# A hybrid encoder block on one NeuronCore: attention copies, query transposes and casts in another order, and a softmax factor made on GpSimd instead of VectorE

## The chip, the cores and the metric

The kernel runs on one core of one Trainium2 chip. The metric is the device time of one execution in microseconds (us), median of three runs.

## What is computed

One layer of a residual block on 512 rows of 1024 values, all in float32 (cut to what matters here):

```
h = rmsnorm(x);  z = h @ W_in            # MLA latents | differential q | k | v
# differential attention, 4 heads of 128, q and k in two maps of 64 each:
logits = q_m . k_m * scale + bias        # m = 0, 1, block-causal mask
probs  = softmax(logits)
attn   = probs[0] - lam * probs[1]
o      = rmsnorm(attn @ v) * (1 - lam_init)
x += concat[MLA heads (8 x 64), differential heads (4 x 128)] @ W_out
x += W_down( silu(causal_conv3(h2 W_gate)) * (h2 W_up) ),  h2 = rmsnorm(x)
x += sigmoid(rmsnorm(x) W_pg) * (p W_pp)
```

The two maps of a differential head are combined before they are multiplied by the values. With e0, e1 the exponentials and s0, s1 their sums over the keys, the kernel forms e0 + e1 * cf with cf = -lam * s0 / s1. That is s0 times the wanted row; the norm that follows removes the factor s0.

## The kernel before, in words

Every matrix product is made three times in reduced-precision float32: each operand is split into a high part (a cast, on ScalarE, line 185 or 150) and a low part (a subtraction, on VectorE, line 186 or 151), and `mm3` (lines 157 to 159) multiplies high by high, high by low and low by high.

TensorE's instructions run in the order in which the code issues them, through the whole kernel. VectorE, ScalarE and GpSimd run in the code's order only inside two regions (`tc.manual_schedule`); between the regions a scheduler of the framework orders them. The first region reaches from the first loads to just before the loop over the differential steps; that loop itself, `for i, (h, t) in enumerate(dslots)`, lies outside it. `tc.issue_after(x)` keeps an instruction behind x.

The stages: projections, then the MLA heads in four pairs `hp`, each in four steps `t` of 128 queries and (t+1)*128 keys, then the differential heads `h` in four steps `t` likewise, then the rest of W_out, the feed-forward part and the gate. While attention waits, TensorE is filled with units of other products: `pump(n)` takes the next n units of `zd_units` (the differential q, k and v) or, later, of `wo_units` (W_out).

An MLA step: `mla_logits` (maxima on VectorE), `mla_exp` (ScalarE), `mla_norm` (sums inverted, P scaled, VectorE), `mla_T` (P transposed on TensorE, then copied from PSUM to SBUF by VectorE or ScalarE, in `probs_T`), `mla_pv` (P times values). At the end of a pair the next pair's first logits follow at once.

A differential step (h, t): `diff_logits` makes the two maps' logits in two PSUM banks out of three (`lg`); VectorE adds the bias, writes the map into one of four SBUF buffers (`pmd`) and finds its row extreme in the same instruction (line 733, shown in the trace as CUSTOM_DVE_ANT_0, here called the maximum), and ScalarE makes the exponential with its sum (line 734). `diff_comb` makes the factor cf and combines the maps (lines 742 to 744). Logits and combination of step i+2 are issued in step i; then `probs_T` transposes step i's map and ScalarE copies it, and `diff_pv` multiplies step i-1 by its values. `diff_T(h, 0)` and `diff_T(h, 1)` transpose a head's queries and keys (TensorE, into one of two banks `tp`) and split them; `y_split` does so for a finished head.

The tiles of W_out are loaded into one of three buffers by SP's queue, cast, and split; a load can start when the low part of the tile that had the buffer is made. `first_hi` loads and casts the first tile in the MLA part (a table `extra` says at which step), `wo_units` the others.

Of the kernel before, what the change touches and what calls it, by code (L numbers as in the profile page):

```python
# [94 lines left out]
def hybrid_block(ctx: ExitStack, tc: tile.TileContext, a: dict, out: bass.AP):  # L95
# [27 lines left out]
    def pt_tile(name):  # L123
        return att.tile([P, T], F32, tag="pt", bufs=2, name=name)
# [10 lines left out]
    def small(name, shape, pool=None):  # L135
        return (pool or atts).tile(shape, F32, name=name)
# [3 lines left out]
    def load_raw(src, n, name):  # L140
        raw = wp["rawpool"].tile([P, 1024], F32, tag="raw", bufs=wp["raw"], name=f"raw_{name}")
        nc.sync.dma_start(raw[:, :n], src)
        return raw
# [51 lines left out]
    V.memset(ones, 1.0)  # L195
    mhalf = small("mhalf", [P, 32], keep)
    V.memset(mhalf, -0.5)
    S.activation(warm[:, :1], ones[:, :1], AF.Exp)
    wps = bank("ob", "warm")
    for i in range(WARM):  # L200
# [199 lines left out]
    def z_flush():  # L400
        while zouts:
            zouts.pop(0)()
# [137 lines left out]
    pump(FILL_QK)  # L540


    def probs_T(pm, n, name, on_act):

        ps = bank("tp", f"pT{name}")
        for j in range(0, n, P):
            TE.transpose(ps[:, j:j + P], pm[:, j:j + P], ident)
        pt = pt_tile("pt")
        if on_act:
            S.copy(pt[:, :n], ps[:, :n])  # L550
        else:
            V.tensor_copy(pt[:, :n], ps[:, :n])
        return pt
# [17 lines left out]
    def mla_logits(hp, t):  # L571

        n, one = (t + 1) * P, t < 2
        r = rq[:, 0, t, 2 * hp:2 * hp + 2]
        sums = sm.tile([P, 3, 2], F32, tag="sums", bufs=4, name="sums")
        nm = sums[:, 0]
        ps, pm = [], []
        for c in range(2):
            qh_, ql_, kh_, kl_ = QT[c]
            if c and one:  # L580
                ps.append(full[:, n:2 * n])
            else:
                full = bank("lg", f"ml{hp}{t}{c}")
                ps.append(full[:, :n])
            mm3(ps[c], [(qh_[:100, tsl[t]], ql_[:100, tsl[t]], kh_[:100, :n], kl_[:100, :n])])
            if not one:
                V.reduce_max(nm[:, c:c + 1], ps[c], axis=AX.X, negate=True)
                V.tensor_tensor(nm[:, c:c + 1], nm[:, c:c + 1], r[:, c:c + 1], op=ALU.mult)
        if one:
            V.reduce_max(nm, full[:, :2 * n].rearrange("p (c k) -> p c k", c=2), axis=AX.X, negate=True)  # L590
            V.tensor_tensor(nm, nm, r, op=ALU.mult)
        mla["lg", hp, t] = ps, nm, r
        for c in range(2):
            if c and one:
                pm.append(pmf[:, n:2 * n])
            else:
                pmf = pm_tile("pm")
                pm.append(pmf[:, :n])
        mla["pm", hp, t] = pm, pmf, sums, one

    def mla_exp(hp, t, c):

        ps, nm, r = mla["lg", hp, t]
        pm, pmf, sums, one = mla["pm", hp, t]
        S.activation(pm[c], ps[c], AF.Exp, bias=nm[:, c:c + 1], scale=r[:, c:c + 1], accum_out=sums[:, 1, c:c + 1])
# [10 lines left out]
    def mla_T(hp, t):  # L616

        n = (t + 1) * P
        pm, pmf, sums, one = mla.pop(("pm", hp, t))
        if one:  # L620
            pt = probs_T(pmf, 2 * n, f"m{hp}{t}", t)
            mla["pt", hp, t] = [pt[:, :n], pt[:, n:2 * n]]
        else:
            mla["pt", hp, t] = [probs_T(pm[c], n, f"m{hp}{t}{c}", c) for c in range(2)]

    def mla_pv(hp, t):

        if t == 0:
            mla["po"] = bank("ob", f"mo{hp}")
        po, pt = mla["po"], mla.pop(("pt", hp, t))  # L630
        for j in range(t + 1):
            for c in range(2):
                TE.matmul(po[64 * c:64 * c + 64, tsl[t]], kv[j][:, 2 * hp + c, 96:], pt[c][:, tsl[j]], start=j == 0, stop=j == t)
        if t == NT - 1 and hp < H // 2 - 1:
            yn = tt(f"ym{hp}")
            S.copy(yn, po)
            ymn.append(yn)
# [53 lines left out]
    def wo_units(kq, dqs, nk):  # L691

        for dq in dqs:
            w = wo_w(kq, dq)
            if kq == 0 and dq + 1 in dqs:
                with tc.issue_after(df["comb"].ins):
                    wo_first[0, dq + 1] = wo_w(0, dq + 1)
            if kq:
                wo2[dq] = w
            steps = [(b, k) for b in (2 * dq, 2 * dq + 1) for k in range(0, nk, 2)]  # L700
            if (kq, dq) == (0, 0):
                steps.sort(key=lambda s: s[1])
            ps = {}
            for b, k in steps:
                if k == 0:
                    ps[b] = bank("acc", f"o{kq}{b}")
                mm3(ps[b], wo_blocks(4 * kq + k, 4 * kq + k + 2, b, w), k == 0, k == nk - 2)
                if k == nk - 2:
                    add_x(b, ps[b])
                yield  # L710
# [27 lines left out]
    def diff_comb(h, t):  # L738

        pms, n, s0, s1 = df["pm", h, t]  # L740
        cf = sm.tile([P, 1], F32, tag="cf", bufs=4, name="cf")
        V.reciprocal(cf, s1)
        V.scalar_tensor_tensor(cf, cf, nlam, s0, op0=ALU.mult, op1=ALU.mult)
        df["comb"] = V.scalar_tensor_tensor(pms[0][:, :n], pms[1][:, :n], cf, pms[0][:, :n], op0=ALU.mult, op1=ALU.add)
        df["pm", h, t] = pms[0]

# [51 lines left out]
    z2_ = []  # L798
    z2_lo = lambda kq: lo(*z2_[kq])

    def first_hi():
        raw = load_raw(a["w_out"][0, 0], 1024, "o00")
        w = [wts.tile([P, 1024], F32R, tag=i, bufs=NW, name=f"{i}_o00") for i in ("hi", "lo")]
        wo_first[0, 0] = w
        z2_.append((*hi(raw, w[0]), w[1]))

    sq, zs = (lambda c, t: lambda: zd_sq(c, t)), (lambda c, t: lambda: zd_scale(c, t))
# [5 lines left out]
        5: [zl(1), sq(0, 3), lambda: zd_root(0)],  # L813
        6: [sq(1, 0), zh(2)],
        7: [zl(2), zh(3)],
        8: [zl(3), sq(1, 1), zs(0, 0), first_hi],
        9: [zl(4), sq(1, 2)],
        10: [sq(1, 3), lambda: zd_root(1), zs(0, 1)],
        11: [zs(0, 2), zs(0, 3)],
        12: [load_x, zs(1, 0), zs(1, 1)],  # L820
        13: [zs(1, 2), zs(1, 3)],
    }
    late = {
        14: [yy(0)],
        15: [yy(1)],
    }
    mla_q(0)
    pump()
# [11 lines left out]
    for hp in range(HP):  # L840
        for t in range(NT):
            i = NT * hp + t
            last = hp == HP - 1
            n = FILL_MLA[hp][t]
            if t:
                mla_norm(hp, t)
            if t < NT - 1:
                mla_logits(hp, t + 1)
            if t == 2:
                for c, (d, m) in enumerate(((diff_T, (0, 0)), (diff_T, (0, 1))) if last else ((mla_q, (2 * hp + 2,)), (mla_k, (2 * hp + 2,)))):  # L850
                    d(*m)
                    mla_exp(hp, t + 1, c)
            elif t < 2:
                for c in range(2):
                    mla_exp(hp, t + 1, c)
            else:
                pump()
                n -= 1
                if last:
                    diff_logits(0, 0)  # L860
                else:
                    mla_q(2 * hp + 3)
                    mla_k(2 * hp + 3)
            if t == 0:
                mla_norm(hp, t)
            for e in extra.get(i, ()):
                e()
            pump(n)
            for e in late.get(i, ()):
                e()  # L870
            mla_T(hp, t)
            z_flush()
            if i:
                mla_pv(*divmod(i - 1, NT))
            if t == 3 and not last:
                mla_logits(hp + 1, 0)
                for c in range(2):
                    mla_exp(hp + 1, 0, c)
    assert next(fill[0], None) is None
    fill[:] = [wo_units(0, range(4), 4)]  # L880
    diff_logits(0, 1)
    mla_pv(HP - 1, NT - 1)
    y_hl(3, mla["po"])
    diff_comb(0, 0)
    diff_T(1, 1)
    y_hl(2, ymn[2])
    diff_comb(0, 1)
    region.__exit__(None, None, None)
    pump()
    for i, (h, t) in enumerate(dslots):  # L890
        if i + 2 < len(dslots):
            diff_logits(*dslots[i + 2])
            diff_comb(*dslots[i + 2])
        pump(FILL_DIFF[h][t])
        df["pt", h, t] = probs_T(df.pop(("pm", h, t)), (t + 1) * P, f"d{h}{t}", True)
        if i:
            diff_pv(*dslots[i - 1])
        if h + 1 < DH and t == 0:
            diff_T(h + 1, 0)
        if h and t == 1:  # L900
            df["scaling"]()
        if t == 3 and h + 2 < DH:
            diff_T(h + 2, 1)
        if h and t == 2:
            y_split(4 + h - 1, df["y", h - 1], ocol, "tp")
        if h and t == 3:
            if h == 2:
                fill.append(wo_units(1, range(2), 2))
# [660 lines left out]
```

## Time and profile before

| what | value |
|---|---|
| median of three runs | 644.52 us (644.42 to 644.86) |
| the profiled execution | 644.82 us, of which the span is 643.0 us |
| TensorE busy in the span | 632.4 us (98%) |
| VectorE busy | 486.9 us (76%) |
| ScalarE busy | 360.2 us (56%) |
| GpSimd busy | 69.2 us (11%) |
| stretch of the differential heads | 157 to 217 us |

Times in the profile are counted from the span's start. In a row of the timeline the first number is the start, the second the duration, both in us; in a row of groups the two numbers behind the bar are the busy time in us and the mean duration of one instruction in ns. PE is TensorE, DVE VectorE, ACT ScalarE, POOL GpSimd, SP the queue of loads. [...]

### The profile page before, as it was taken

The numbers are of one execution on the slowest core, as the hardware profiler recorded it, in microseconds if no ns is written. First come the engines' busy times: TensorE is split into PE (matmuls) and PEld (weight loads), VectorE is DVE, ScalarE is ACT, GpSimd is POOL, SyncE is SP. The second block draws the span as 40 slices with busy tenths as digits, with TensorE's granted clock in tenths as the row PEclk, the third lists the DMA queues.
The fourth block names the chain that finished last, engine by engine and source line by source line (L and its number), as shares of the span: only waits on it lengthen the run. The fifth ranks groups of instructions, "written<-read, shape, count | busy, mean of one in ns | idle before, by whom it ended". The sixth has DMA issues, their size and how long they took to land.

```text
span 643.0 us, 10203 instructions
## 1 busy us (share of the span) xinstructions
PE 632.4 (98%) x3900; PEld 556.2 (87%) x3900; DVE 486.9 (76%) x870; ACT 360.2 (56%) x629; POOL 69.2 (11%) x94
## 2 busy tenths in 40 slices
PE   8999999999999999999999999999999999999997
PEld 8988888876777887889999999999999999988886
DVE  6889667887898678988876767676767777759844
ACT  7896567666667355557555545545454545637111
POOL 1514103030000130001000000000100000000000
PEclk9999999999999999999999999999999999999999
DMA  8241612330221437546865656464646554532021
GB/s 304 100 165 37 182 62 66 99 130 2 66 85 49 164 132 228 148 95 157 208 197 117 184 124 199 117 180 116 180 115 182 118 177 115 181 130 66 27 88 50
DMA packets 29912, 82.63 MB, mean 129 GB/s; under 512 B 3100, under 2 KB 4124, under 8 KB 29736
## 3 DMA queue, kind: packets, MB, share of 16 engines
q1 hardware_dynamic: 23816, 69.17, 32.3%
q0 software_dynamic: 5616, 12.33, 11.3%
q8 instruction: 31, 0.51, 0.3%
q10 hardware_dynamic: 432, 0.49, 0.2%
q14 instruction: 17, 0.14, 0.1%
HBM read 77.77 MB, written 5.52 MB: 130 GB/s over the span
## 4 chain that ended last, share of the span: by engine, by line
PE 86%; DVE 7%; ACT 3%; issue 2%; DMA 1%; ACTq 0%; DVEq 0%; SPq 0%
PE dn L157 6%; PE dn L158 6%; PE dn L159 6%; PE gx L159 4%; PE gx L158 4%; PE gx L157 4%; PE zd L157 3%; PE zd L159 3%; PE zd L158 3%; PE g L157 3%; PE g L158 3%; PE g L159 3%; PE pg L159 2%; PE pg L158 2%; PE pg L157 2%; PE o L157 2%
## 5 line engine op out<-in xcount | busy, mean ns | idle before, releaser
L954 DVE TENSOR_TENSOR wSl<-rS,wSh 128x1024 fp32r<-128x1024 f32 x21 | 25.7, 1224 | 43.4 <-ACT wSh L950 43.2
L157 PE MATMUL dn<-ah,hi_dn 128*128 128x512 f32 x144 | 56.2, 391 | 0.0
L158 PE MATMUL dn<-al,hi_dn 128*128 128x512 f32 x144 | 56.2, 391 | 0.0
L159 PE MATMUL dn<-ah,lo_dn 128*128 128x512 f32 x144 | 56.0, 389 | 0.0
L1071 POOL DMA_DIRECT2D rS<-in_w_gu x19 | 22.7, 1194 | 250.2 <-DVE cv L1239 129.9
L950 ACT CAST wSh<-rS 128x1024 fp32r<-128x1024 f32 x21 | 22.0, 1047 | 35.7 <-PE gy L158 35.4
L157 PE MATMUL zd<-hi_d,xh 128*128 128x512 f32 x96 | 39.1, 407 | 0.0
L158 PE MATMUL zd<-lo_d,xh 128*128 128x512 f32 x96 | 37.6, 392 | 0.0
L682 DVE TENSOR_TENSOR x<-x,dn 128x512 f32<-128x512 f32 x44 | 29.9, 679 | 6.1 <-PE dn L159 6.1
L954 DVE TENSOR_TENSOR wTl<-rA,wTh 128x1024 fp32r<-128x1024 f32 x19 | 23.3, 1225 | 13.7 <-ACT wTh L950 13.2
L159 PEld LDWEIGHTS dn<-ah,lo_dn 128*128 128x128 f32 x144 | 27.0, 188 | 5.8
L157 PEld LDWEIGHTS dn<-ah,hi_dn 128*128 128x128 f32 x144 | 27.1, 188 | 5.1
L158 PEld LDWEIGHTS dn<-al,hi_dn 128*128 128x128 f32 x144 | 27.1, 188 | 5.0
L954 DVE TENSOR_TENSOR wAl<-rA,wAh 128x1024 fp32r<-128x1024 f32 x21 | 25.6, 1217 | 2.7 <-ACT wAh L950 2.7
L950 ACT CAST wAh<-rA 128x1024 fp32r<-128x1024 f32 x21 | 22.1, 1050 | 9.7 <-DMA rA<-in_w_gu 9.5
L1242 ACT ACTIVATE cv<-cv 128x512 f32<-128x512 f32 x22 | 13.9, 630 | 23.9 <-DVE cv L1239 23.8
L157 PE MATMUL g<-b2h,wAh 128*128 128x256 f32 (+1 forms) x88 | 26.4, 300 | 0.5 <-ACT g L1195 0.5
L157 PE MATMUL o<-yh,hi_o 128*128 128x512 f32 x64 | 26.8, 419 | 0.0
L734 ACT ACTIVATE pmd<-pmd,nmd 128x128 f32<-128x128 f32 (+3 forms) x32 | 17.9, 560 | 15.1 <-DVE nmd L733 15.0
L159 PE MATMUL g<-b2h,wAl 128*128 128x256 f32 (+1 forms) x88 | 26.2, 297 | 0.0
L158 PE MATMUL g<-b2l,wAh 128*128 128x256 f32 (+1 forms) x88 | 26.2, 297 | 0.0
L1462 ACT ACTIVATE sg<-sg 128x512 f32<-128x512 f32 (+1 forms) x9 | 5.3, 584 | 36.8 <-DVE sg L1461 36.8
(475 smaller groups left out, 2219.1 us busy)
## 6 DMA issues: line engine op xcount, KB each, us to landing
rA<-in_w_gu SPq DMA_DIRECT2D x22, 512.0 KB, 3.7
rS<-in_w_gu SPq DMA_DIRECT2D x22, 512.0 KB, 3.7
rS<-in_w_gu POOLq DMA_DIRECT2D x19, 512.0 KB, 6.1
raw_dn<-in_w_down SPq DMA_DIRECT2D x18, 512.0 KB, 5.9
raw_d<-in_w_d SPq DMA_DIRECT2D x12, 512.0 KB, 3.4
r<-in_w_gu SPq DMA_DIRECT2D x19, 256.0 KB, 5.9
raw_o<-in_w_out SPq DMA_DIRECT2D x8, 512.0 KB, 3.6
rS_pg<-in_w_pg SPq DMA_DIRECT2D x6, 512.0 KB, 4.1
```

Of the source, the lines that this page charges most:

```text
L157: TE.matmul(ps, xh, wh, start=first and i == 0, stop=False, skip_group_check=again)
L158: TE.matmul(ps, xh, wl, start=False, stop=False, skip_group_check=again)
L159: TE.matmul(ps, xl, wh, start=False, stop=last and i == n - 1, skip_group_check=again)
L682: V.tensor_tensor(xb(b), xb(b), ps, op=ALU.add)
L734: S.activation(pm[:, :n], pm[:, :n], AF.Exp, bias=nm, scale=-1.0, accum_out=s0 if m == 0 else s1)
L950: S.copy(h_, src)
L954: V.tensor_tensor(l_, src, _f32(h_), op=ALU.subtract)
L1071: nc.gpsimd.dma_start(sums[f].rearrange("p (i c) -> p i c", i=2), a["w_gu"][f][:, :2048].rearrange("p (i c) -> p i c", i=2)[:, :, :512], a ...
L1242: S.activation(cv, cv, AF.Silu)
L1462: S.activation(sg, sg, AF.Sigmoid)
```

## The change

Four edits in the attention part. The copies of an MLA step's transposed P are split off `probs_T` (`probs_out`, `mla_pt`); at the end of a head pair they are issued behind the next pair's logits, maxima and exponentials. A differential head's queries are transposed two heads ahead, at step 1, instead of one head ahead at step 0. Casts and splits are set elsewhere: the second tile of W_out is loaded and cast at step 12 of the MLA part, its low part made at the region's end, and y 1's split moves behind the last MLA step. The factor cf is made by GpSimd: s1 to the power of -1, times -lam, times s0, in three instructions of one column, where VectorE had a reciprocal and one fused product.

```
+    mone = small("mone", [P, 1])
+    V.memset(mone, -1.0)
...
     def diff_comb(h, t):
         pms, n, s0, s1 = df["pm", h, t]
         cf = sm.tile([P, 1], F32, tag="cf", bufs=4, name="cf")
-        V.reciprocal(cf, s1)
-        V.scalar_tensor_tensor(cf, cf, nlam, s0, op0=ALU.mult, op1=ALU.mult)
+        G.tensor_tensor(cf, s1, mone, op=ALU.pow)
+        G.tensor_tensor(cf, cf, nlam, op=ALU.mult)
+        G.tensor_tensor(cf, cf, s0, op=ALU.mult)
         df["comb"] = V.scalar_tensor_tensor(pms[0][:, :n], pms[1][:, :n], cf, pms[0][:, :n], op0=ALU.mult, op1=ALU.add)
...
-            if kq == 0 and dq + 1 in dqs:
+            if kq == 0 and 0 < dq and dq + 1 in dqs:
                 with tc.issue_after(df["comb"].ins):
                     wo_first[0, dq + 1] = wo_w(0, dq + 1)
...
-    def first_hi():
+    def first_hi(dq):
...
-        12: [load_x, zs(1, 0), zs(1, 1)],
+        12: [load_x, zs(1, 0), zs(1, 1), lambda: first_hi(1)],
...
     late = {
         14: [yy(0)],
-        15: [yy(1)],
     }
...
             mla_T(hp, t)
-            z_flush()
+            if t < 3:
+                mla_pt(hp, t)
+                z_flush()
             if i:
                 mla_pv(*divmod(i - 1, NT))
-            if t == 3 and not last:
-                mla_logits(hp + 1, 0)
-                for c in range(2):
-                    mla_exp(hp + 1, 0, c)
+            if t == 3:
+                if not last:
+                    mla_logits(hp + 1, 0)
+                    for c in range(2):
+                        mla_exp(hp + 1, 0, c)
+                mla_pt(hp, t)
+                z_flush()
...
     diff_logits(0, 1)
     mla_pv(HP - 1, NT - 1)
+    y_hl(1, ymn[1])
+    diff_comb(0, 0)
     y_hl(3, mla["po"])
-    diff_comb(0, 0)
     diff_T(1, 1)
     y_hl(2, ymn[2])
     diff_comb(0, 1)
+    z2_lo(5)
     region.__exit__(None, None, None)
...
-        if h + 1 < DH and t == 0:
-            diff_T(h + 1, 0)
+        if t == 0 and h == 0:
+            diff_T(1, 0)
+        if t == 1 and h + 2 < DH:
+            diff_T(h + 2, 0)
```

Where instructions stand before and after, at three places. First VectorE at the border of MLA head pairs 2 and 3: `pt<-pTm` is the copy of the last step's P, `sums<-ml` the maximum of the next pair's steps 0 and 1 (names carry buffer numbers at their end). Before:

```order
L552 COPY pt_1597<-pTm230_1592 128x512
L590 TENSOR_REDUCE sums_1612<-ml300_1613 128x2
L591 TENSOR_TENSOR sums_1612<-sums_1612,rq_505 128x2
L590 TENSOR_REDUCE sums_1625<-ml310_1626 128x2
L591 TENSOR_TENSOR sums_1625<-sums_1625,rq_505 128x2
L613 RECIPROCAL sums_1612<-sums_1612 128x2
```

The same place in the changed kernel:

```order
L596 TENSOR_REDUCE sums_1610<-ml300_1611 128x2
L597 TENSOR_TENSOR sums_1610<-sums_1610,rq_507 128x2
L558 COPY pt_1623<-pTm230_1594 128x512
L596 TENSOR_REDUCE sums_1627<-ml310_1628 128x2
L597 TENSOR_TENSOR sums_1627<-sums_1627,rq_507 128x2
L619 RECIPROCAL sums_1610<-sums_1610 128x2
```

The copy has moved between the two maxima. Second, VectorE at differential step (1, 2): `pmd,nmd<-dl` is a map's maximum (a row with `nmd` alone reads it out), `cf` the factor, `pmd<-pmd,cf` the combination, `st<-d1T2` the split of head 2's keys. Before:

```order
L186 TENSOR_TENSOR st_123<-d1T2_2049,st_123 128x512
L733 ISA pmd_2061,nmd_2062<-dl120_2057,strip_939 128x384
L733 ISA nmd_2062 128x1
L733 ISA pmd_2069,nmd_2070<-dl121_2065,strip_939 128x384
L733 ISA nmd_2070 128x1
L742 RECIPROCAL cf_2073<-s1_2056 128x1
L743 SCALAR_TENSOR_TENSOR cf_2073<-cf_2073,nlam_227,s0_1968 128x1
L744 SCALAR_TENSOR_TENSOR pmd_2061<-pmd_2069,cf_2073,pmd_2061 128x384
```

After, VectorE:

```order
L747 ISA pmd_2076,nmd_2077<-dl120_2072,strip_941 128x384
L747 ISA nmd_2077 128x1
L186 TENSOR_TENSOR st_125<-d1T2_2064,st_125 128x512
L747 ISA pmd_2084,nmd_2085<-dl121_2080,strip_941 128x384
L747 ISA nmd_2085 128x1
L759 SCALAR_TENSOR_TENSOR pmd_2076<-pmd_2084,cf_2088,pmd_2076 128x384
```

and GpSimd, for the steps (1, 2) and (1, 3), with the power of head 0's norm (`ro`) between them:

```order
L756 TENSOR_TENSOR cf_2088<-s1_2071,mone_88 128x1
L757 TENSOR_TENSOR cf_2088<-cf_2088,nlam_229 128x1
L758 TENSOR_TENSOR cf_2088<-cf_2088,s0_1981 128x1
L781 TENSOR_TENSOR ro_2115<-mo_2114,mhalf_86 128x4
L756 TENSOR_TENSOR cf_2136<-s1_2119,mone_88 128x1
```

The factor's two rows have left VectorE, and three stand on GpSimd. Third, ScalarE around differential step (2, 3): `sqo` and `yd` read the finished head 1, `pk` are the casts of p and of W_pp, `pmd,s0` and `pmd,s1` the exponentials of the two maps. Before:

```order
L758 ACTIVATE sqo_2287<-do1_2143 128x512
L759 COPY yd1_2286<-do1_2143 128x512
L188 ACTIVATE st_123<-d0T3_2297,dcol_119 128x512
L734 ACTIVATE pmd_2309,s0_2146<-pmd_2309,nmd_2310 128x512
L922 CAST pk_2599<-raw_pT_2600 128x1024
L922 CAST pk_2599<-raw_pp0_2604 128x1024
L734 ACTIVATE pmd_2317,s1_2304<-pmd_2317,nmd_2318 128x512
```

After:

```order
L773 ACTIVATE sqo_2307<-do1_2153 128x512
L774 COPY yd1_2306<-do1_2153 128x512
L945 CAST pk_2617<-raw_pT_2618 128x1024
L945 CAST pk_2617<-raw_pp0_2622 128x1024
L748 ACTIVATE pmd_2322,s0_2163<-pmd_2322,nmd_2323 128x512
L748 ACTIVATE pmd_2330,s1_2317<-pmd_2330,nmd_2331 128x512
```

Both casts now stand ahead of both exponentials, and the split of head 3's queries has left this place for an earlier one.

More of the change, by code (lines that the diff above doesn't have):

```diff
@@ L540, in hybrid_block, with probs_T @@
     pump(FILL_QK)
-    def probs_T(pm, n, name, on_act):
+    def probs_T(pm, n, name):
         ps = bank("tp", f"pT{name}")
@@ L547, in probs_T, with probs_out @@
             TE.transpose(ps[:, j:j + P], pm[:, j:j + P], ident)
+        return ps
+    def probs_out(ps, n, on_act):
         pt = pt_tile("pt")
@@ L620, in mla_T, with mla_pt @@
         if one:
-            pt = probs_T(pmf, 2 * n, f"m{hp}{t}", t)
+            mla["pT", hp, t] = [probs_T(pmf, 2 * n, f"m{hp}{t}")]
+        else:
+            mla["pT", hp, t] = [probs_T(pm[c], n, f"m{hp}{t}{c}") for c in range(2)]
+    def mla_pt(hp, t):
+        n, ps = (t + 1) * P, mla.pop(("pT", hp, t))
+        if t < 2:
+            pt = probs_out(ps[0], 2 * n, t)
             mla["pt", hp, t] = [pt[:, :n], pt[:, n:2 * n]]
         else:
-            mla["pt", hp, t] = [probs_T(pm[c], n, f"m{hp}{t}{c}", c) for c in range(2)]
+            mla["pt", hp, t] = [probs_out(ps[c], n, c) for c in range(2)]
     def mla_pv(hp, t):
@@ L799, in hybrid_block @@
     z2_lo = lambda kq: lo(*z2_[kq])
-    def first_hi():
-        raw = load_raw(a["w_out"][0, 0], 1024, "o00")
-        w = [wts.tile([P, 1024], F32R, tag=i, bufs=NW, name=f"{i}_o00") for i in ("hi", "lo")]
-        wo_first[0, 0] = w
+    def first_hi(dq):
+        raw = load_raw(a["w_out"][0, dq], 1024, f"o0{dq}")
+        w = [wts.tile([P, 1024], F32R, tag=i, bufs=NW, name=f"{i}_o0{dq}") for i in ("hi", "lo")]
+        wo_first[0, dq] = w
         z2_.append((*hi(raw, w[0]), w[1]))
@@ L815, in hybrid_block @@
         7: [zl(2), zh(3)],
-        8: [zl(3), sq(1, 1), zs(0, 0), first_hi],
+        8: [zl(3), sq(1, 1), zs(0, 0), lambda: first_hi(0)],
         9: [zl(4), sq(1, 2)],
@@ L894, in hybrid_block @@
         pump(FILL_DIFF[h][t])
-        df["pt", h, t] = probs_T(df.pop(("pm", h, t)), (t + 1) * P, f"d{h}{t}", True)
+        df["pt", h, t] = probs_out(probs_T(df.pop(("pm", h, t)), (t + 1) * P, f"d{h}{t}"), (t + 1) * P, True)
         if i:
             diff_pv(*dslots[i - 1])
-        if h + 1 < DH and t == 0:
-            diff_T(h + 1, 0)
+        if t == 0 and h == 0:
+            diff_T(1, 0)
+        if t == 1 and h + 2 < DH:
+            diff_T(h + 2, 0)
         if h and t == 1:
```

## The prediction

> **What bounds the kernel now.** I read the page first, then a table by stretch, then TensorE's waits, then VectorE's waits and both engines' timelines in the differential heads.
>
> ```profile
> PE 632.4 (98%) x3900; PEld 556.2 (87%) x3900; DVE 486.9 (76%) x870; ACT 360.2 (56%) x629; POOL 69.2 (11%) x94
> PE 86%; DVE 7%; ACT 3%; issue 2%; DMA 1%; ACTq 0%; DVEq 0%; SPq 0%
> 157.00:217.00 60.00, 58.39 (x359) 46.22 (x358) 52.55 (x147) 38.01 (x95) 3.02 (x3) 1.00 0.20 63
> PE dl L159 <- DVE st L189: 0.9, 2, 0.6
> PE mo L633 <- DVE pt L552: 0.7, 1, 0.7
> PE pTd L547 <- ACT pt L550: 0.5, 1, 0.5
> PE pTm L547 <- DVE pm L614: 0.3, 1, 0.3
> DVE cf L742 <- ACT pmd L734: 3.7, 6, 1.0
> ```
>
> TensorE is busy 98% of the span and carries 86% of the chain, so a stretch matters only where TensorE waits. The third line is the differential heads: 60 us, TensorE 58.39 busy, VectorE 52.55 of 60 (88%, the fullest stretch of that engine). TensorE's named waits that the change could remove are the next four lines, together 2.4 us. That is the most its moves can bring. The last line is what matters for the second edit: VectorE already stands 3.7 us at the reciprocal, waiting for the second map's exponential.
>
> **The loop that the factor lies in.** One step of head 1 (384 keys) reads so, VectorE first, ScalarE below:
>
> ```profile
> 175.12 0.55 DVE L733 CUSTOM_DVE_ANT_0 pmd<-dl,strip 128x384 f32<-128x384 f32 x1
> 176.58 0.17 DVE L742 RECIPROCAL cf<-s 128x1 f32<-128x1 f32 x1 [0.90 <-ACT pmd L734]
> 177.03 0.62 DVE L744 SCALAR_TENSOR_TENSOR pmd<-pmd,cf 128x384 f32<-128x384 f32 x1
> 175.85 0.60 ACT L734 ACTIVATE pmd<-pmd,nmd 128x384 f32<-128x384 f32 x1
> 176.36 0.19 ACT L734 ACTIVATION_READ_ACCUMULATOR pmd<-pmd,nmd 128x1 f32 x1
> ```
>
> Second map's maximum at 175.12, its exponential, the sum out at 176.55, reciprocal 176.58, combination 177.03: the factor costs 0.48 us after the sum. The maps have four buffers, and in both orders the second maximum of a step stands behind the combination of the step before (it takes that buffer). So maximum, exponential, factor, combination, next maximum is a serial loop, run 14 times from step (0,2) to (3,3), and what the factor gains in length each turn gains, unless VectorE has other work queued between maximum and combination.
>
> **The factor on GpSimd.** Per step VectorE loses a reciprocal and a product (0.38 us busy); GpSimd gets a power and two products of one column, and VectorE's combination now waits for GpSimd with everything behind it in VectorE's queue.
>
> ```profile
> L766 POOL TENSOR_TENSOR ro<-mo,mhalf 128x4 f32<-128x4 f32 x4 | 4.0, 1006 | 79.7 <-DVE mo L765 79.7
> L165 POOL TENSOR_TENSOR rl<-rs_m,mhalf 128x8 f32<-128x8 f32 x1 | 1.7, 1652 | 0.8 <-DVE rs_m L164 0.8
> L381 POOL TENSOR_TENSOR kr<-za,rc_k 128x32 f32<-128x32 f32 x4 | 1.3, 325 | 0.7 <-ACT za L369 0.7
> L382 POOL TENSOR_TENSOR krt<-za,rs_k 128x16 f32<-128x16 f32 x4 | 1.1, 277 | 0.0
> 16.66 1.03 POOL L293 TENSOR_SCALAR rs_k<-rs_k 128x64 f32<-128x64 f32 x1
> 15.80 0.77 POOL L292 TENSOR_TENSOR rs_k<-rtab,rows 128x64 f32<-128x64 f32 x1
> 218.85 1.01 POOL L766 TENSOR_TENSOR ro<-mo,mhalf 128x4 f32<-128x4 f32 x1 [7.09 <-DVE mo L765]
> 219.89 0.69 DVE L769 TENSOR_TENSOR yd<-yd,ro 128x512 f32<-128x512 f32 x1 [1.18 <-POOL ro L766]
> ```
>
> No row has one column. Power: 1.006 at four, 1.652 at eight, 0.16 a column, so 0.52 at one (bounds: 0.36, the line's start, and 1.01, no fall below four). Product: 0.277 at 16, 0.325 at 32, so 0.23 at one (bounds 0 and 0.28). A dependent GpSimd pair starts 0.09 after the first ends (15.80+0.77 to 16.66); I take 0.08, the same from ScalarE, and 0.03 back to VectorE (219.86 to 219.89). Factor: 0.08+0.52+0.08+0.23+0.08+0.23+0.03 = 1.25 us (bounds 0.63 and 1.84), against 0.48: 0.77 more a step. I take 1.25, since two lines through measured rows give it.
>
> ```profile
> L151 DVE TENSOR_TENSOR lo_o<-raw_o,hi_o 128x1024 fp32r<-128x1024 f32 x7 | 8.5, 1217 | 0.0
> L682 DVE TENSOR_TENSOR x<-x,o 128x512 f32<-128x512 f32 x12 | 8.1, 682 | 0.1
> L733 DVE CUSTOM_DVE_ANT_0 pmd<-dl,strip 128x512 f32<-128x512 f32 x8 | 5.4, 679 | 0.0
> L733 DVE CUSTOM_DVE_ANT_0 pmd<-dl,strip 128x128 f32<-128x128 f32 x6 | 1.7, 287 | 0.4
> L744 DVE SCALAR_TENSOR_TENSOR pmd<-pmd,cf 128x512 f32<-128x512 f32 x4 | 3.0, 750 | 0.1
> L744 DVE SCALAR_TENSOR_TENSOR pmd<-pmd,cf 128x128 f32<-128x128 f32 x4 | 1.4, 351 | 0.1
> L189 DVE SCALAR_TENSOR_TENSOR st<-d0T,dcol,st 128x512 fp32r<-128x512 f32 x3 | 2.2, 746 | 0.1
> L734 ACT ACTIVATE pmd<-pmd,nmd 128x512 f32<-128x512 f32 x8 | 5.8, 724 | 2.3 <-DVE nmd L733 2.3
> L734 ACT ACTIVATE pmd<-pmd,nmd 128x128 f32<-128x128 f32 x6 | 2.4, 400 | 4.8 <-DVE nmd L733 4.8
> raw_o<-in_w_out SPq DMA_DIRECT2D x8, 512.0 KB, 3.6
> 162.21 0.55 DVE L733 CUSTOM_DVE_ANT_0 pmd<-dl,strip 128x384 f32<-128x384 f32 x1
> 210.53 0.69 DVE L733 CUSTOM_DVE_ANT_0 pmd<-dl,strip 128x512 f32<-128x512 f32 x1
> 214.58 0.60 PE L547 MATMUL pTd<-ident,pmd 128*128 128x128 f32 x4
> ```
>
> From a second maximum to its combination: maximum 0.29/0.42/0.55/0.68 for 128/256/384/512 keys, 0.03, exponential with the sum read 0.50/0.60/0.71/0.82, factor 1.25: 2.08/2.31/2.55/2.79 us (the middle sizes interpolated), 0.13 to 0.19 more where the first maximum stands directly ahead and its exponential is still running. Behind it I add, in the new order, the rows between combination and next second maximum; queued VectorE instructions start 0.08 before the one ahead ends, so a 1.22 us split takes 1.14, a sum into x 0.60, a combination 0.27/0.41/0.53/0.67, a query split 0.67.
>
> (0,2) 2.68+0.53+0.67 = 3.88. (0,3) 2.79+0.67+0.67 = 4.13. (1,0) 2.08+0.27+split 1.14+first maximum 0.34 = 3.83. (1,1) 2.47+0.41+0.47+0.60 = 3.95. (1,2) 4.86: 3.01, since ScalarE's cast of w_out tile 11 stands ahead of the exponentials and its load (3.6 us after the split that frees the buffer) lands late, then 0.53+0.60+0.60 and small. (1,3) 2.79+0.67+0.67+0.21 = 4.34. (2,0) 2.27+0.27+1.14+0.60+1.14+0.67+0.34 = 6.43. (2,1) 2.47+0.41+0.47+0.60 = 3.95. (2,2) 0.47+1.14+0.60+1.14 = 3.35 of VectorE's own work (maximum, split, sum, split) covers the loop's 2.55, then 0.53+0.60+0.60 and small: 5.16, where the factor's 0.77 costs nothing. (2,3) 4.73: 4.06 because the casts of pT and w_pp now stand ahead of both exponentials and the second load again follows a late split, then 0.67. (3,0) 2.08+0.27+0.60+0.34+0.67 = 3.96. (3,1) 2.31+0.41 = 2.72. (3,2) 2.55+0.53+0.60+0.60+0.08 = 4.36. Together 56.3 us, against 48.3 now (162.21 to 210.53).
>
> The start: in the region ahead y 1's split ends at 157.9, and behind it stand the combination of (0,0), 0.27, y 3's split, the key split of head 1, y 2's split, 0.60 each, the combination of (0,1), 0.41, and the split of w_out tile 1, 1.14, which so ends at 161.5; the first maximum of (0,2) follows, and the second at 161.91 (162.21 now). Then (3,3) comes at 218.2, its combination ends 2.79+0.75 later at 221.75, and the last transposes, at 214.58 now, start at 221.80: **7.2 us later**. TensorE's order behind them is unchanged, and nothing there catches up. On the way TensorE waits where it had not: logits have three banks, so the second map of a step waits for the first maximum of the step before, about 2 us at (2,0); the transposes of head 3's keys wait for y 4's split, about 2.5 us; the last transposes about 2. The four waits of today are inside these.
>
> GpSimd's queue holds little else there: the four-column power of a finished head (1.01) stands ahead of the factor of step 3 and ends, by the walk, before that sum is out. SP's queue keeps its order.
>
> **The moves.** Maxima ahead of P copies, at the heads' borders:
>
> ```profile
> 136.96 0.42 DVE L590 TENSOR_REDUCE sums<-ml 128x2 f32<-128x256 f32 x1
> 137.72 0.69 DVE L590 TENSOR_REDUCE sums<-ml 128x2 f32<-128x512 f32 x1
> 155.45 1.09 PE L633 MATMUL mo<-pt,kvb 128*64 128x128 f32 x16 [0.74 <-DVE pt L552]
> 153.47 0.60 ACT L185 CAST yh<-ym 128x512 fp32r<-128x512 f32 x1
> ```
>
> The maximum at 136.96 starts 0.13 after VectorE is free: it waits for the logits, not for the copy, so going first gains nothing. The copy (0.69) then falls between 136.96 and 137.72 and delays the second maximum to 138.11 and the reciprocal behind it by 0.22; where only one filler unit follows, at head pair 3, TensorE's transposes come 0.22 later. At the end of the MLA part the copy no longer stands behind y 1's split: values times P at 155.15 instead of 155.45. But y 1's cast, free at 153.47 now, moves behind the exponentials to 156.6, its split ends 157.9, and the second block of the first output unit wants it at 157.5: 0.45 back. Net at the next logits +0.15, which the sum's start has in it. Query transposes two heads ahead: the same eight on TensorE, the loop above decides whether they wait. Set casts: w_out tile 1 is cast at step 12, its load keeps its place on SP's queue; one memset at the start, under the first loads. I cost these at nothing.
>
> [...] GpSimd beside a VectorE instruction with two SBUF operands:
>
> ```profile
> 13.75 1.36 POOL L290 TENSOR_TENSOR rc_k<-rtab,rows 128x64 f32<-128x64 f32 x1 [12.44 <-DMA rtab<-in_rope]
> 13.70 1.23 DVE L212 TENSOR_TENSOR xq<-xq 128x1024 f32<-128x1024 f32 x1
> ```
>
> GpSimd's 1.36 ends 0.18 after VectorE's 13.70+1.23, while 0.77 suffices a row later. [...] By rows, splits of w_out run beside the factor at (2,1) and (2,2): up to 0.4 and 0.6 us more, 1.0 in all, which I leave out of the sum and put in the range.
>
> **Rivals.** (a) Faster. The factor is hidden: the combination is wanted two steps later, and VectorE is 0.38 us a step lighter. Then the 2.4 us of waits go, and 642.1 results. It decides where the factor is under about 0.65 us (7.2 over the 12 turns that feel it is 0.60 a turn). The 3.7 us of waits at L742 speak against it, one-column powers of 0.36 for it. Chance 0.08.
> (b) Within 0.2%, about 644.5: a factor near 0.65, loop and gain cancel. 0.05.
> (c) Much slower: power stays at 1.01 for one column. 12 turns of 0.49 more, 5.9: 657.6. Chance 0.07.
> (d) TensorE's clock falls in the new waits. Granted clock is 1.00 in the stretch above with waits up to 0.6, so nothing here shows it; two falls that each halve 3.4 us of work would add 3.4: 655. [...] 0.05.
>
> **How the numbers follow.** Profiled execution: 643.0 span, 644.82 in all, 0.30 over the median 644.52. 644.82+7.2-0.3 = 651.7. Forecast 0.75 for the serial loop with a factor of 0.9 to 1.6 us: 12 x 0.35 off either way gives 647.5 to 656. The range takes in the lower half of what lies between (b) and it, and part of (c) and (d): 645.5 to 656.5. Measured differences under 0.2% (1.3 us) are no change. Faster 0.08, same 0.05, slower 0.87.
>
> **What would show it.** Between 157 and 225 VectorE's waits name GpSimd's factor, some 10 us or more; GpSimd's three rows near 0.52, 0.23, 0.23; TensorE's waits there grow by 7, first on VectorE's maxima and y 4's split; from the last transposes on, all is shifted alike. Wrong if one-column GpSimd instructions are far shorter, or if waits of VectorE do not reach TensorE.

## The result, and the profile after

The changed kernel takes 654.85 us (median of four runs, 654.44 to 655.33), the kernel before 644.69 us on the same chip. The ratio is 1.0156, with a 95% interval from 1.0143 to 1.0169: 10.2 us slower. The forecast was 651.7 us, range 645.5 to 656.5, slower with a chance of 0.87. The profiled execution took 654.53 us with a span of 652.8. One execution of an experiment told below (one product less) took 2.2 ms for a reason that nothing on record shows; neither its time nor its trace is used.

Two rows of the page, busy time and chain, then the stretch of the differential heads (same columns as before):

```profile
PE 636.5 (98%) x3900; PEld 557.6 (85%) x3900; DVE 481.1 (74%) x839; ACT 358.6 (55%) x629; POOL 84.7 (13%) x142
PE 82%; DVE 7%; ACT 4%; DMA 2%; issue 2%; POOL 1%; ACTq 0%; SPq 0%; DVEq 0%
157.00:225.00 68.00, 60.12 (x348) 46.20 (x347) 47.52 (x115) 37.23 (x96) 18.30 (x48) 1.00 0.15 47
```

The stretch has grown from 60 to 68 us. VectorE has less to do in it (47.52 us instead of 52.55), and that helps nobody. TensorE now stands still where it ran through: 68 less 60.12 is 7.9 us, against 1.6 before. The waits of TensorE, then of VectorE, then GpSimd's groups say who waits for whom:

```profile
PE o L157 <- DVE x L696: 2.5, 1, 2.5
PE d1T L729 <- DVE yh4l L189: 2.3, 1, 2.3
PE dl L157 <- DVE nmd L747: 1.6, 2, 1.1
PE do L767 <- ACT yd L774: 0.7, 1, 0.7
PE pTm L549 <- DVE pm L620: 0.4, 1, 0.4
```

```profile
DVE pmd L759 <- POOL cf L758: 16.6, 13, 2.5
DVE yd L784 <- POOL ro L781: 2.2, 3, 1.1
```

```profile
L756 POOL TENSOR_TENSOR cf<-s,mone 128x1 f32<-128x1 f32 x16 | 8.9, 555 | 57.5 <-ACT pmd L748 57.5
L757 POOL TENSOR_TENSOR cf<-cf,nlam 128x1 f32<-128x1 f32 x16 | 4.2, 265 | 1.3
L758 POOL TENSOR_TENSOR cf<-cf,s 128x1 f32<-128x1 f32 x16 | 3.0, 190 | 1.3
```

TensorE waits for VectorE; VectorE waits 16.6 us, at 13 of its combinations, for GpSimd's factor. The step of head 1 with 384 keys, which the prediction showed, now reads so (VectorE, ScalarE, GpSimd):

```profile
178.01 0.55 DVE L747 CUSTOM_DVE_ANT_0 pmd<-dl,strip 128x384 f32<-128x384 f32 x1
181.08 0.62 DVE L759 SCALAR_TENSOR_TENSOR pmd<-pmd,cf 128x384 f32<-128x384 f32 x1 [2.51 <-POOL cf L758]
177.64 1.05 ACT L150 CAST hi_o<-raw_o 128x1024 fp32r<-128x1024 f32 x1 [1.33 <-DMA raw_o<-in_w_out]
179.71 0.19 ACT L748 ACTIVATION_READ_ACCUMULATOR pmd<-pmd,nmd 128x1 f32 x1
179.97 0.54 POOL L756 TENSOR_TENSOR cf<-s,mone 128x1 f32<-128x1 f32 x1 [3.47 <-ACT pmd L748]
180.59 0.19 POOL L757 TENSOR_TENSOR cf<-cf,nlam 128x1 f32<-128x1 f32 x1
180.86 0.19 POOL L758 TENSOR_TENSOR cf<-cf,s 128x1 f32<-128x1 f32 x1
```

The sum is out at 179.90 (179.71 + 0.19), the combination starts at 181.08: the factor takes 1.18 us, where it took 0.48. ScalarE's cast stands ahead of the exponentials and waits for its load, as forecast for this step.

The table gives the time from one second maximum to the next, in us, from the starts of its rows in five kernels (the fourth and the fifth are experiments told below):

| second maximum of step | before | forecast walk | changed | two more products | fifth buffer alone |
|---|---|---|---|---|---|
| (0,2) to (0,3) | 3.42 | 3.88 | 3.87 | 4.41 | 3.81 |
| to (1,0) | 3.63 | 4.13 | 4.12 | 4.66 | 4.20 |
| to (1,1) | 2.78 | 3.83 | 3.83 | 4.38 | 3.81 |
| to (1,2) | 3.08 | 3.95 | 3.88 | 4.42 | 3.94 |
| to (1,3) | 3.66 | 4.86 | 4.88 | 5.31 | 4.81 |
| to (2,0) | 3.82 | 4.34 | 4.43 | 4.90 | 4.43 |
| to (2,1) | 4.39 | 6.43 | 6.38 | 5.63 | 6.40 |
| to (2,2) | 4.37 | 3.95 | 4.01 | 5.06 | 4.03 |
| to (2,3) | 5.92 | 5.16 | 5.60 | 5.61 | 5.59 |
| to (3,0) | 4.57 | 4.73 | 4.37 | 5.25 | 2.12 |
| to (3,1) | 2.78 | 3.96 | 3.97 | 4.64 | 4.24 |
| to (3,2) | 2.23 | 2.72 | 2.94 | 3.48 | 2.73 |
| to (3,3) | 3.67 | 4.36 | 4.40 | 4.94 | 4.37 |
| sum | 48.3 | 56.3 | 56.7 | 62.7 | 54.5 |

The first and the last of the changed kernel's fourteen rows:

```profile
162.31 0.55 DVE L747 CUSTOM_DVE_ANT_0 pmd<-dl,strip 128x384 f32<-128x384 f32 x1
218.99 0.68 DVE L747 CUSTOM_DVE_ANT_0 pmd<-dl,strip 128x512 f32<-128x512 f32 x1
```

The loop alone has grown by 8.4 us. Of the 9.7 us by which the last transposes are late (224.25 instead of 214.58), 0.1 lies ahead of it, and 1.2 arise behind it, in the last step:

```profile
220.20 0.69 DVE L784 TENSOR_TENSOR yd<-yd,ro 128x512 f32<-128x512 f32 x1 [0.53 <-POOL ro L781]
220.81 0.68 DVE L696 TENSOR_TENSOR x<-x,o 128x512 f32<-128x512 f32 x1
221.86 0.75 DVE L759 SCALAR_TENSOR_TENSOR pmd<-pmd,cf 128x512 f32<-128x512 f32 x1 [0.37 <-POOL cf L758]
221.54 0.50 PE L157 MATMUL o<-yh,hi_o 128*128 128x512 f32 x1 [2.51 <-DVE x L696]
223.03 0.49 PE L549 MATMUL pTd<-ident,pmd 128*128 128x128 f32 x3
223.36 0.61 PE L767 MATMUL do<-zd,pt 128*128 128x128 f32 x4
223.81 0.60 PE L679 MATMUL yT<-ident,yd 128*128 128x128 f32 x4
224.25 0.60 PE L549 MATMUL pTd<-ident,pmd 128*128 128x128 f32 x4
```

The last unit of W_out waits 2.51 us for its bank, which a sum into x frees; that sum stands in VectorE's queue behind the scaling of head 2, which waits for GpSimd's four-column power. The transposes of steps (3, 2) and (3, 3) stand behind that unit on TensorE. So the last ones start 1.64 us after their combination is done (222.61), though nothing in them needs the unit.

In the kernel before, VectorE took that sum first and the scaling behind it, and TensorE's next weight load waited only 0.15 us for it. From the combination's end to the last transposes it was 0.98 us (213.60 to 214.58):

```profile
211.13 0.68 DVE L682 TENSOR_TENSOR x<-x,o 128x512 f32<-128x512 f32 x1
211.79 0.69 DVE L769 TENSOR_TENSOR yd<-yd,ro 128x512 f32<-128x512 f32 x1
212.85 0.75 DVE L744 SCALAR_TENSOR_TENSOR pmd<-pmd,cf 128x512 f32<-128x512 f32 x1
```

So the scheduler has turned the two round. Among the traces used here, it did so in all those with GpSimd's factor and the combination in its old place, and in none of the others. No run turns this pair alone.

### The profile page after: what moved, and what is told of

The parts are those of the page before. It is cut to its first block, busy times and chain, and to the rows that moved or that the text cites. A ratio compares the mean times of both kernels' runs of the same rounds, so it can differ in the third digit from the quotient of the medians.

```text
span 652.8 us, 10225 instructions
## 1 busy us (share of the span) xinstructions
PE 636.5 (98%) x3900; PEld 557.6 (85%) x3900; DVE 481.1 (74%) x839; ACT 358.6 (55%) x629; POOL 84.7 (13%) x142
## 4 chain that ended last, share of the span: by engine, by line
PE 82%; DVE 7%; ACT 4%; DMA 2%; issue 2%; POOL 1%; ACTq 0%; SPq 0%; DVEq 0%
PE dn L157 6%; PE dn L158 6%; PE dn L159 6%; PE gx L159 4%; PE gx L158 4%; PE gx L157 4%; PE zd L157 3%; PE zd L159 3%; PE zd L158 3%; PE g L157 3%; PE g L159 3%; PE g L158 3%; PE pg L159 2%; PE pg L157 2%; PE pg L158 2%
## 5 line engine op out<-in xcount | busy, mean ns | idle before, releaser
L611 ACT ACTIVATE pm<-ml,sums,rq 128x128 f32<-128x128 f32 (+3 forms) x32 | 19.6, 616 | 16.3 <-DVE sums L597 10.7
```

## The experiments

Ratios are to runs of the kernel before on the same chip, with 95% intervals.

**Which edit.** The factor back on VectorE with all moves kept, and the factor alone on the kernel before:

```
# the first, on the changed kernel; the second is the reverse, on the kernel before
-        G.tensor_tensor(cf, s1, mone, op=ALU.pow)
-        G.tensor_tensor(cf, cf, nlam, op=ALU.mult)
-        G.tensor_tensor(cf, cf, s0, op=ALU.mult)
+        V.reciprocal(cf, s1)
+        V.scalar_tensor_tensor(cf, cf, nlam, s0, op0=ALU.mult, op1=ALU.mult)
```

> The changed kernel with the factor back on VectorE (reciprocal and one fused product), all moves kept. Theory 1, the serial loop of the factor: nearly all of the 10.2 us is the factor's length, so 643 to 646 us. Rival 2, the moves (copies behind the next pair's maxima, transposes two heads ahead, casts ahead of the exponentials) carry the loss: 652 to 655 us. In between, say 648 to 650, both have a share.

> The kernel before with nothing changed but the factor (three GpSimd instructions). Theory 1: the loop takes the same 0.72 us a step more here, in about 12 turns, and the last output unit's bank wait comes with it: 653 to 656 us. Rival 2, the moves: within 1 us of 644.7. If the moves help or cost something of their own, the two runs of this pair show it: the sum of their differences from the kernel before against the 10.2 us of both together.

Measured: 645.63 us with the moves alone (ratio 1.0017, 1.0008 to 1.0027), 656.48 us with the factor alone (1.0181, 1.016 to 1.0202). So the factor by itself costs as much as the whole change (12.0 us against 10.2, with overlapping intervals), half a microsecond more than I expected at most. The differences of the two runs, 1.1 and 12.0 us, do not add up to the 10.2; why is not shown. The moves by themselves cost about 1 us: with the factor on VectorE, TensorE's longest wait lies at the transposes of step (2, 3), and in the same step a cast stands ahead of the second map's exponential:

```profile
204.13 0.66 PE L549 MATMUL pTd<-ident,pmd 128*128 128x128 f32 x4 [1.40 <-ACT pt L556]
199.23 1.05 ACT L944 CAST pk<-raw_pp 128x1024 fp32r<-128x1024 f32 x1 [0.42 <-DMA raw_pp<-in_w_pp]
```

The first row's wait is 0.47 us in the kernel before (its row at 203.16), and the cast there does not wait for its load. That the cast is the cause of the 1 us was not tried by itself.

**How long the chain.** If the factor's length is what counts, the loss must follow it in both directions. First the product of s0 and -lam taken ahead of the power, so that one product less stands behind the sum; then two products more:

```
# one product less behind the sum (c0 is a second column of the cf tile)
+        G.tensor_tensor(c0, s0, nlam, op=ALU.mult)
         G.tensor_tensor(cf, s1, mone, op=ALU.pow)
-        G.tensor_tensor(cf, cf, nlam, op=ALU.mult)
-        G.tensor_tensor(cf, cf, s0, op=ALU.mult)
+        G.tensor_tensor(cf, cf, c0, op=ALU.mult)
# two more
         G.tensor_tensor(cf, cf, nlam, op=ALU.mult)
+        G.tensor_tensor(cf, cf, mone, op=ALU.mult)
+        G.tensor_tensor(cf, cf, mone, op=ALU.mult)
         G.tensor_tensor(cf, cf, s0, op=ALU.mult)
```

> The changed kernel with the product of s0 and -lam made by GpSimd ahead of the power, while the second map's exponential runs, so that one product stands behind the sum instead of two: the chain from the sum to the combination is 0.27 us shorter (0.19 for the product and 0.08 for the hand-over), with as many GpSimd instructions. Theory 1: about 12 turns of 0.27 = 3.2 us less, 651.6 us (650.5 to 652.5). [...] Rival 4, what counts is only that VectorE's order waits for another engine at all, not how long: no change.

> The changed kernel with two more products of one column by -1 (which cancel) in the factor: the chain is 0.54 us longer. Theory 1: 12 turns of 0.54 = 6.5 us more, 661.3 us (660 to 662.5). Rival 4: no change, 654.9. [...]

> The kernel with one product taken ahead of the power once more, for an undisturbed trace: 652.5 to 654 us as measured. By theory 1 the intervals between second maxima are each 0.27 us shorter, 3.2 us in all from (0, 2) to (3, 3), wherever VectorE's order is the same as in the changed kernel; what of this does not reach the end must be a wait of its own in the last steps, where the scheduler's order differs (three places), and it shows as a wait of TensorE.

Measured: 661.34 us with two more (1.0254, 1.023 to 1.0277), against an expected 661.3. The table shows it turn by turn: 0.4 to 0.9 us more in ten of the thirteen. In the three from (2, 0) to (2, 3) the scheduler set splits of W_out in other turns; together they take 16.30 us instead of 15.99, and VectorE waits for the factor in each of them (0.9 to 2.3 us). The loop is 6.0 us longer, not 6.5, so that the time meets the forecast so closely is in part luck. With one less, 653.00 and, again, 653.31 us (1.0132 and 1.0134), only 1.5 to 1.9 us under 654.85 where 3.2 were expected. The loop did shorten: its sum is 53.9 us against 56.7, 2.7 less. In the profiled execution the rest was given back at the end, by something that no expectation of these runs had put there:

```profile
220.90:224.30 3.40, 3.40 (x15) 3.02 (x14) 1.31 (x3) 0.48 (x1) 0.00 (x0) 0.51 0.00 0
```

This is a stretch of the kernel with one product less; the third number from the end is the granted clock. Behind a wait of 2.2 us for the same bank TensorE ran 3.4 us at a clock of 0.51. From the last second maximum to the last transposes it is 6.89 us here (217.48 to 224.37), against 5.26 in the changed kernel's first trace: 1.6 us given back. In another execution of the changed kernel, with the same fall (below), it is 6.89 too.

**The end of the chain.** The last unit behind the last transposes; then dummy work in the wait; and the changed kernel once more:

```
# unit behind the transposes: the last row of FILL_DIFF
-(1, 1, 2, 2)
+(1, 1, 1, 0)
# kept busy, at step (3, 2), written out for that step
-        pump(2)
+        pump(1)
+        ps = bank("lg", "busy")
+        for k in range(16):
+            TE.transpose(ps[:, :P], ident, ident)
+        pump(1)
```

> The changed kernel with the last unit of W_out in the differential heads issued behind the last transposes instead of ahead of them (fill of steps (3, 2) and (3, 3): 1 and 0 units instead of 2 and 2, of which the last two found nothing left). TensorE waits 2.5 us for that unit's bank in the changed kernel, with the transposes of steps (3, 2) and (3, 3) behind it. If this wait is the part that my sum missed, the transposes no longer stand behind it and the last ones start right behind their combination, at 222.7 instead of 224.25: 1.2 to 1.6 us less, 653.3 to 653.7 us. If the loop alone sets the end, no change: 654.9.

> The changed kernel with 16 transposes of the identity into a free logits bank (1.8 us of TensorE) issued ahead of the last unit of W_out, for whose bank TensorE waits 2.5 us. They do no part of the computation and lie inside that wait. If the fall of the granted clock after this wait costs the end (half speed for 3.4 us is 1.7 us of work, in runs where it falls), the runs lose up to 1.7 us of time and the mean granted clock rises from about 0.994 towards 0.997: 653.5 to 654.3 us. If it lies in time that is waited anyway, 654.4 to 655.3 us as the changed kernel.

> The changed kernel itself, as the control of these runs: 654.85 us within 0.7, with granted clocks of 0.994 to 0.998.

Measured: 653.86 us (1.0141, 1.0123 to 1.016), 654.06 us (1.0147, 1.0133 to 1.0161) and, for the changed kernel again, 656.00 us (1.0174, 1.016 to 1.0188). With the unit moved, the last transposes start 3.77 us after the last second maximum (219.25 to 223.02) instead of 5.26 (218.99 to 224.25): 1.5 us less, as expected, so the bank's wait is what my sum lacked. There too the clock halves, at 222.8 (0.52 over 222.9 to 226.3). The time is 1.0 us under the first median of the changed kernel and 2.1 under the second.

The other two show the price of such a fall. Three executions follow: the stretch behind the bank's wait in the changed kernel; the same stretch in the changed kernel again, with an earlier one; and the kernel kept busy, the whole end and an earlier stretch. The clock is the third number from the end.

```profile
222.00:225.40 3.40, 3.40 (x27) 3.06 (x25) 2.16 (x5) 1.44 (x3) 0.00 (x0) 1.00 0.00 0
```

```profile
222.00:225.40 3.40, 3.40 (x15) 3.00 (x14) 1.63 (x4) 0.48 (x1) 0.00 (x0) 0.51 0.00 0
194.90:198.30 3.40, 3.40 (x14) 2.81 (x13) 2.48 (x7) 3.04 (x6) 0.73 (x3) 0.52 0.69 242
```

```profile
219.00:226.00 7.00, 6.18 (x48) 5.43 (x45) 4.12 (x9) 2.85 (x8) 1.49 (x4) 1.00 0.08 17
203.10:206.50 3.40, 3.40 (x11) 2.68 (x10) 2.12 (x8) 2.47 (x8) 1.64 (x4) 0.61 0.00 0
```

From the last second maximum to the last transposes it is 5.26 us at full clock, 6.89 with the fall (218.65 to 225.54), and 5.27 with TensorE kept busy (218.32 to 223.59). So the fall there cost 1.6 us. In this one trace with dummy work inside the wait none came there. The first trace of the changed kernel had none without such work, so this alone does not show that the work prevents it; against the changed kernel measured beside it (656.00) the runs are 1.9 us faster, and the two intervals just touch. Falls within the loop (the second rows of the last two blocks, and one more in the third trace, at 183.4, with 0.54 over 183.7 to 187.1) cost nothing here: the sum over the fourteen maxima is 56.68 us in all three. By my reading that is because VectorE sets the pace there and TensorE has time to spare (in the first trace 60.12 us busy of 68).

**What closes the loop.** A fifth map buffer alone; then the fifth buffer with each combination one step later, forced behind the second maximum of the next step, with the factor on GpSimd, on VectorE, and on the kernel before without any of the moves:

```
-PM = 4
+PM = 5
...
             diff_logits(*dslots[i + 2])
-            diff_comb(*dslots[i + 2])
+        if 0 < i < len(dslots) - 1:
+            diff_comb(*dslots[i + 1])
...
+        with tc.issue_after(df["max"].ins):     # the latest second maximum
             df["comb"] = V.scalar_tensor_tensor(...)
```

> The changed kernel with the fifth map buffer and nothing else. VectorE's order stays the same but for one pair in the last steps, with every combination ahead of the next second maximum. If the loop closes through the buffer (the maximum waits for the map that the combination frees), it opens: 646 to 650 us. If it closes through VectorE's own order (the maximum stands behind a combination that waits for GpSimd), nothing changes: 654 to 655.5 us. I expect the second.

> The changed kernel with the factor still on GpSimd, a fifth map buffer, and each combination issued one step later, behind the second maximum of the next step, so that no maximum waits for a combination and VectorE has two maxima to do while GpSimd makes the factor. Theory 1, latency in a serial loop: VectorE's 16.6 us of waits for the factor nearly go and the loss with them, 644 to 648 us (a second maximum now waits for the transposes two steps back, which may cost some). [...] Rival 2, the moves: 653 to 655.

> The same fifth buffer and later combination, with the factor on VectorE (reciprocal and fused product). It is the control of the run with GpSimd: by theory 1 both come within 1.5 us of each other, 643 to 647 us; if GpSimd's factor still costs 0.7 us a step, this one is 8 to 10 us ahead.

> The kernel before with only the fifth map buffer and each combination behind the second maximum of the next step; factor on VectorE, none of the moves. If the gain of the later combination over the kernel before (1.2 us with all moves) is the reordering's own, this gives 643 to 644 us. If it came from the moves, 644.5; if the moves cost here what they cost with the combination in its old place (1.1 us), 642 us.

The buffer alone: 652.53 us (1.0124, 1.011 to 1.0138). VectorE still waits 14.4 of the 16.6 us for the factor, so the queue's order closes the loop. It gained 2.3 us on the changed kernel's first median (3.5 on the repeat), 1.5 more than I allowed. The loop's share, 2.2 us, comes from one place: with a buffer free, the scheduler set one second maximum, at (3, 0), ahead of the combination. There the table has 2.12 instead of 4.37, and nothing else moved by more than 0.3. VectorE's rows of the changed kernel and of this one:

```profile
205.13 0.29 DVE L747 CUSTOM_DVE_ANT_0 pmd<-dl,strip 128x128 f32<-128x128 f32 x1
206.78 0.75 DVE L759 SCALAR_TENSOR_TENSOR pmd<-pmd,cf 128x512 f32<-128x512 f32 x1 [1.28 <-POOL cf L758]
207.68 0.29 DVE L747 CUSTOM_DVE_ANT_0 pmd<-dl,strip 128x128 f32<-128x128 f32 x1
```

```profile
204.68 0.28 DVE L747 CUSTOM_DVE_ANT_0 pmd<-dl,strip 128x128 f32<-128x128 f32 x1
204.97 0.28 DVE L747 CUSTOM_DVE_ANT_0 pmd<-dl,strip 128x128 f32<-128x128 f32 x1
206.23 0.75 DVE L759 SCALAR_TENSOR_TENSOR pmd<-pmd,cf 128x512 f32<-128x512 f32 x1 [0.97 <-POOL cf L758]
```

One turn out of thirteen, opened by the scheduler's choice, and it shows what the others need. With all of them opened: 642.89 us with the factor on GpSimd (0.9979, 0.997 to 0.9989), 643.34 us with it on VectorE (0.998, 0.9971 to 0.999). The same three GpSimd instructions run, and cost nothing. VectorE's and TensorE's waits with GpSimd's factor, from 157 us on:

```profile
DVE pmd L760 <- POOL cf L758: 0.9, 3, 0.4
```

```profile
PE o L158 <- DVE yh1l L186: 0.2, 1, 0.2
```

0.9 us instead of 16.6, and no other wait of TensorE of 0.2 us or more is named in that stretch. That GpSimd's instructions by themselves slow VectorE is out as the main cause: the instructions are the same, the loss is gone.

The kernel before with only the buffer and the later combination has the lowest time: 642.47 us (0.9968, 0.9956 to 0.9981), 2.1 us faster than before, and nearest to the 642 expected if the moves cost something here too. It beats both kernels. Its interval overlaps those of the two runs with the moves, so all that is shown is that the moves gain nothing here.

## Why the prediction was right, and where its sum was short

*The loop and its waits: right.* VectorE's waits were to name GpSimd's factor, some 10 us or more: 16.6. TensorE's waits were to grow by 7, first on maxima and on y 4's split: the two are 1.6 and 2.3 us, and all idle time in the stretch is 6.3 us more. The reason that I gave for the order, "it takes that buffer", was not the one that counts: with a fifth buffer twelve of the thirteen turns stayed closed, by VectorE's order. The walk's 56.3 us measured 56.7, and no turn missed by more than 0.45 either way, so the close sum owes a little to misses that cancel.

*The factor: right within 0.07 us.* Power 0.52, measured 0.54 in the step shown and 0.555 on average; products 0.23, measured 0.19; in all 1.25, measured 1.18. The line through four and eight columns held at one, so the rivals of a short factor (a, b) and of a power of 1.01 (c) both fell.

*GpSimd beside a split: right in kind, small in size.* Beside the split at (2, 2) GpSimd's first product took 1.01 us instead of 0.19, and ended 0.05 after the split:

```profile
200.18 1.01 POOL L757 TENSOR_TENSOR cf<-cf,nlam 128x1 f32<-128x1 f32 x1
199.92 1.22 DVE L151 TENSOR_TENSOR lo_o<-raw_o,hi_o 128x1024 fp32r<-128x1024 f32 x1
```

VectorE then waited 0.35 us for the factor, and that turn is 0.44 longer than walked (5.60 against 5.16); I had kept 0.6 for it in the range. At (2, 1), for which I had kept 0.4, the factor's three rows are 0.62, 0.19 and 0.19, and the turn is 0.06 longer than walked. Both were my estimates, from one pair of rows before the change (GpSimd's 1.36 beside VectorE's 1.23); what holds GpSimd up in such a place was not shown.

*The moves: right that they gain nothing, too kind in size.* At the head pairs' border TensorE waits 0.4 us for the scaled P instead of 0.3 (forecast 0.22 more), and the moves alone cost 1.1 us where I had 0.15 outside the casts' loads. The turn with the cast at (1, 2) came as walked (4.88 for 4.86), that with the casts at (2, 3) 0.36 shorter.

*The start: 0.4 us later than walked.* The second maximum of (0, 2) stands at 162.31, walked at 161.91. At the first MLA logits, ahead of every edit but the memset, the profiled execution is already 0.52 later (69.91 before, 70.43 after). Over all the traces that point moves by nearly 2 us from one execution to the next (69.67 to 71.62), so this need not be the change's.

*The term that failed: from the last combination to the last transposes.* The walk had them start 0.05 us after the combination's end; they start 1.64 after it. I had written that TensorE's order behind the loop was unchanged and that the last transposes would wait about 2 us, and took this wait for one on their own data. It is the wait of the unit ahead, for a bank that a sum frees, which stands behind a scaling, which stands behind GpSimd's four-column power. What put the sum behind the scaling is the scheduler's order on VectorE, which the walk did not price. The edit to TensorE's issue order showed 1.5 us of it. Account of the 2.45 us between 221.80 and 224.25: 0.40 start, 0.38 turns, 0.08 from maximum to combination, 1.59 here. In all the profiled execution is 2.5 us over the walk. The median is 3.15 over the forecast: it lies 0.3 over the profiled execution, where I had it 0.3 under. The range held this; the size was short, 7.2 us forecast for 10.2 measured.

*The clock: a rival of 0.05 that was half right.* I wrote that two falls would each halve 3.4 us and together add 3.4. The falls of the runs are of that size (0.51 and 0.52 over 3.4 us in the repeat of the changed kernel). The profiled execution has none in this stretch (1.00), but its fellow runs show mean clocks of 0.994, against 0.998, and those of the repeat 0.990 to 0.993. The step that was off is where I looked for the price: a fall in the loop cost nothing in these traces, one behind it 1.6 us.

## What to carry to other kernels

Price an instruction that is moved to an idle engine by the latency that it adds between its input and its consumer, and ask what else stands behind the consumer in its queue. If the consumer's queue has the next turn's work behind it, the loop pays in full, however idle the engine was (here 8.4 us, with GpSimd busy 13% of the span); issuing the consumer one turn later, behind that work, with one more buffer, made the same slow factor free (642.89 us against 654.85). When a wait is added, also look at what TensorE has queued behind the waiting instruction and does not need it: there the wait delays that work too (here by 1.5 us), and in some executions here the clock fell behind it (0.51 over 3.4 us, 1.6 us of time). And look whether the scheduler has set other work in another order, which the changed lines do not show.

## What the runs showed of the hardware that I had not expected

TensorE's granted clock halved behind a single wait of 1.04 us. In the kernel with two more products a stretch with that wait, TensorE busy 2.36 of 3.4, is followed by one at half clock (0.50), and that by one at full clock (1.00):

```profile
173.20:176.60 3.40, 2.36 (x11) 1.59 (x10) 2.77 (x7) 1.48 (x6) 0.33 (x2) 1.00 0.16 35
176.70:180.10 3.40, 3.40 (x15) 2.79 (x13) 2.04 (x6) 1.63 (x4) 0.90 (x5) 0.50 0.28 111
180.10:183.50 3.40, 3.40 (x21) 2.52 (x22) 0.58 (x2) 2.22 (x6) 1.30 (x5) 1.00 0.00 0
```

This trace has three such falls, with clocks of 0.50, 0.51 and 0.50 over the 3.4 us from 176.7, 197.2 and 227.9. The clock's mean over the microsecond in which each begins gives its place (0.83 is 0.66 us at full and the rest at half):

```profile
176.00:177.00 1.00, 1.00 (x4) 0.86 (x5) 0.03 (x1) 1.00 (x4) 0.63 (x2) 0.83 0.57 205
197.00:198.00 1.00, 1.00 (x4) 0.77 (x4) 0.96 (x1) 0.69 (x1) 0.92 (x2) 0.57 0.13 33
227.00:228.00 1.00, 1.00 (x5) 0.82 (x5) 0.34 (x1) 0.00 (x0) 0.47 (x3) 0.93 0.00 0
```

So 176.66, 197.14 and 227.86: 20.48 and 30.72 apart. Worked out the same way, the two falls of the repeated changed kernel (clock 0.87 over 194 to 195 and 0.52 over 222 to 223, so 194.74 and 222.04) lie 27.30 apart. These distances are near 6, 9 and 8 times 3.41 us. That step is an estimate of mine from the places of these five falls alone; what sets the places was not shown. The same kernel can show falls in one execution and none in the next: the changed kernel's profile with waits of 2.5 and 2.3 us has none in the differential heads (a clock of 1.00 over 157 to 225), its repeat, with waits of 2.5 and 2.4, has two. How much idle time it takes was not settled.
